# The second feed-forward of a two-layer network, computed as one quad over all 1024 tokens with a down projection of its own

## The chip, the cores and the metric

The kernel runs on one core of a Trainium2 chip. The metric is the device time of one execution in microseconds (us), the median of several runs. The profiler's trace of one execution gives the *span*, from the first to the last instruction. The engines are TensorE (PE, with its weight loads as PEld), VectorE (DVE), ScalarE (ACT), GpSimd (POOL) and SyncE (SP), which issues nearly all DMA transfers. SBUF is the on-chip memory, PSUM the accumulators that TensorE writes, DRAM the memory off the core.

## What is computed

Two layers, each with a mixing part and a gated feed-forward, and a norm at the end:

```python
    for layer in range(DEPTH):
        ...
        h = h + g1 * o_lat
        h = h + g2 * swiglu(rms_norm(h, norm_g[layer, 1]) * (1.0 + sc2) + sh2,
                            ffn_w_gate[layer], ffn_w_up[layer], ffn_w_down[layer])
        ...
    return rms_norm(h, final_g)
```

`h` is 1024 tokens by 1024 features in float32. `swiglu(x)` is `(silu(x Wg) * (x Wu)) Wd` with 2816 hidden units. Only the second layer's feed-forward, the last thing before the final norm, is changed in earnest.

## The kernel before

**Float32 by three products.** A float32 operand is *cut* into two halves: ACT casts the high half (`split` and `cut`, the cast) and DVE subtracts it to get the low half (names that end in `l`). `mm3` (lines 155 to 157) then issues three matmuls for one: high by high, high by low, low by high.

**Seven products for eight.** Gate and up projections are taken over two by two blocks by Winograd's form of Strassen's identity. A is the weight, in blocks of 128 hidden units by 512 input features (gate and up side by side); B is the normed input, in blocks of 512 features by half of the tokens. Four weight combinations S1 to S4 and four input combinations T1 to T4 are formed. One *step* takes a pair of hidden tiles (2 x 128 units; `NP` = 11 pairs), does the products A11 B11, S2 T2, A12 B21, S3 T3, S1 T1, A22 T4 and S4 B22, adds them up on DVE into the four blocks C, and `hidden` multiplies silu(gate) by up.

**Two token groups.** In the second feed-forward `FF = Quad(1, h, 256, ...)` goes over 512 tokens at a time: `X0` holds the operands of tiles 0 to 3, `X1` those of tiles 4 to 7. A token half is 256 columns, so a product is 24 matmuls of 256 columns. There are `NS` = 22 steps: the weights of all 11 pairs are loaded by SP, combined on POOL (`form`, lines 1312 to 1321, written in place over the raw blocks) and cut (`cut`, line 1327) once for each group. Six cuts of a step have their low half on DVE, that of A22 on POOL. The operands of `X1` (norm, transposes by TensorE, the T combinations and seven cuts) are made in `side1` during the steps 7 to 10 of the first group.

**The down projection inside the step.** `downs` of step s - 1 runs in the middle of step s: 4 token tiles x 2 column halves x 2 hidden tiles x 3 = 48 matmuls of 512 columns. Each pair of down weights is loaded as `wd`, multiplied by the gain `g2` on POOL (line 1302) and cut. DVE adds the PSUM tile `pd` to `h` (line 1364), which stays in SBUF.

**Before and behind.** The layer's gated mixing output (`pgl` matmuls of 512 columns, lines 2020 to 2037) comes just ahead. `ahead` starts the feed-forward's operands in its last quarter. Behind the last step `finish_row` takes the row norm and writes the output, one token tile at a time.

**Order.** Every engine works through its own instructions in order, and a wait holds up all that stand behind it. A scheduler sets this order when the program is built, by what depends on what and its own costs; SP's queue of transfers is one of those orders.

Of the kernel before, what the change touches and what calls it, by code (L numbers as in the profile page):

```python
# [11 lines left out]
F32 = mybir.dt.float32  # L12
# [8 lines left out]
P = 128  # L21
# [70 lines left out]
def build_(tc, A, out):  # L92
# [61 lines left out]
    def mm3(o, ah, al, bh, bl, first, last):  # L154
        nc.tensor.matmul(o, ah, bh, start=first, stop=False)  # L155
        nc.tensor.matmul(o, ah, bl, start=False, stop=False)  # L156
        return nc.tensor.matmul(o, al, bh, start=False, stop=last)  # L157
# [1274 lines left out]

    mix_evac(8, 0, early[0])
# [300 lines left out]
    # context: final state of both directions by pairwise combination  # L1734
# [136 lines left out]
    # within-chunk part  # L1871
# [121 lines left out]
    hp = popen("h", "right")  # L1993
    h = [hp.tile([P, D], F32, name=f"hb{i}") for i in range(8)]
    for i in range(8):
        nc.sync.dma_start(h[i], hdram[i])
    xpa = popen("ffxA", "right")
    FF = Quad(1, h, 256, xpa, popen("raw", "right"))
    X0 = ColumnOperands(FF, (0, 1, 2, 3), True)
    X1 = ColumnOperands(FF, (4, 5, 6, 7), False)  # L2000
    def ahead(i, part):
        if (i, part) == (3, 1):
            FF.load(0)
            X0.prep()
        if (i, part) == (4, 1):
            X0.column(0, gp)
            X0.column(1, gp)
            FF.form(0, "S3")
            FF.form(0, "S2")
        for k in {(5, 0): (0, 1), (5, 1): (2, 3), (6, 0): (4, 5), (6, 1): (6, 7)}.get((i, part), ()):  # L2010
            X0.turn(k)
            if k < 6:
                X0.column(k + 2, gp)
        if (i, part) == (6, 0):
            X0.cut("B11")
            X0.form("T1", nc.vector)
        if (i, part) == (7, 0):
            X0.form("T2", nc.vector)
            X0.form("T3", nc.gpsimd)
            X0.cut("B21")  # L2020
            X0.form("T4", nc.gpsimd)

    for cb in range(4):
# [18 lines left out]
        wl_ = wn  # L2042
    pclose("glu")
    pclose("ssmA")
# [1 line left out]
    FF.begin()  # L2046
    FF.g2 = FF.fq.tile([P, D], F32, name="g2r")
    nc.sync.dma_start(FF.g2, row(1, 5, 0))
# [92 lines left out]
```

## Time and profile before

| | before |
|---|---|
| time, median of 3 runs | 2802.89 us (2801.14 to 2805.78) |
| span of the profiled execution | 2800.7 us |
| busy: PE, DVE, POOL, ACT | 2551.2, 2062.8, 1256.8, 1109.9 us |
| mean granted TensorE clock | 0.962 |
| second feed-forward: last `pgl` matmul to the end | 2042.5 to 2800.7 us, 758.2 us |

The span is one execution and 2.2 us under the median of the runs. A busy time is a sum over the whole program and says nothing of one stage, so the stages are read one by one below. Granted clock 1.00 is full speed.

### The profile page before, as it was taken

What the parts mean: (1) busy time and instruction counts of PE and PEld (TensorE: products, weight loads), DVE (VectorE), ACT (ScalarE), POOL (GpSimd) and SP (SyncE); (2) the same over time, 40 slices, a digit from 0 to 9 for tenths busy, and PEclk for the clock granted to TensorE, in tenths of its full rate; (3) what the DMA queues carried; (4) which work ended last, traced back from release to release, by engine and by line L of the source; (5) the groups of instructions that cost most, each with busy time, mean ns of one, the idle gap of its engine ahead of it and who ended that gap; (6) DMA issues with size and microseconds to landing.
All of it is one profiled execution on the core that took longest, in us unless ns stands there. A gap on an engine that the chain in (4) does not pass through costs nothing.

```text
span 2800.7 us, 40131 instructions
## 1 busy us (share of the span) xinstructions
PE 2551.2 (91%) x15300; PEld 2208.7 (79%) x15300; DVE 2062.8 (74%) x3302; ACT 1109.9 (40%) x1944; POOL 1256.8 (45%) x1084
## 2 busy tenths in 40 slices
PE   7999999988998989889999976499989999889998
PEld 4788777777887879778888863398879998789997
DVE  3545786797888778797766869822298889888887
ACT  4242662363433434333323391421243345443343
POOL 1212111334665654566434567411155554665553
PEclk9999999999999999989999997799999999999999
DMA  6731345333333324433364247441032222233222
GB/s 242 196 104 45 108 138 164 98 126 137 112 107 99 120 86 167 156 100 105 98 186 149 82 161 235 156 143 61 1 98 98 99 91 91 83 121 106 91 97 70
DMA packets 262338, 330.84 MB, mean 118 GB/s; under 512 B 67713, under 2 KB 197553, under 8 KB 261761
## 3 DMA queue, kind: packets, MB, share of 16 engines
q1 hardware_dynamic: 259008, 318.51, 35.2%
q0 software_dynamic: 3136, 9.77, 1.1%
q8 instruction: 120, 1.97, 0.3%
q14 instruction: 74, 0.60, 0.1%
HBM read 285.22 MB, written 48.12 MB: 119 GB/s over the span
## 4 chain that ended last, share of the span: by engine, by line
PE 47%; DVE 33%; ACT 7%; POOL 5%; issue 5%; DMA 3%; SPq 0%; ACTq 0%; POOLq 0%; DVEq 0%
PE pd L155 5%; PE pd L156 5%; PE pd L157 5%; DVE sg L1350 5%; POOL wr L1318 3%; DVE SA L1861 3%; DVE hidl L152 2%; DVE S2l L1327 2%; PE pft L1960 2%; PE pgl L157 2%; PE pgl L156 2%; PE pgl L155 2%; PE pS L157 2%; PE pS L155 2%; DVE A12l L1327 2%
## 5 line engine op out<-in xcount | busy, mean ns | idle before, releaser
L1312 POOL TENSOR_TENSOR ws<-wr 128x1024 f32<-128x1024 f32 x42 | 108.3, 2578 | 251.2 <-DVE S1l L1327 170.0
L1318 POOL TENSOR_TENSOR wr<-wr 128x1024 f32<-128x1024 f32 x40 | 96.3, 2408 | 276.9 <-DVE A11l L1327 276.9
L1327 ACT CAST S4h<-wr 128x1024 fp32r<-128x1024 f32 x43 | 45.1, 1049 | 421.7 <-PE pd L157 421.7
L155 PE MATMUL pd<-W0h,hidh 128*128 128x512 f32 x396 | 163.3, 412 | 47.3 <-DVE c L1396 30.9
L1350 DVE TENSOR_TENSOR sg<-sg,c 128x320 f32<-128x320 f32 (+1 forms) x176 | 191.4, 1088 | 4.9 <-ACT sg L1349 4.6
L1302 POOL TENSOR_TENSOR wd<-wd,g2r 128x1024 f32<-128x1024 f32 x66 | 185.1, 2825 | 16.4 <-DMA wd<-in_ffn_w_down 16.4
L149 ACT CAST hidh<-sg 128x320 fp32r<-128x320 f32 (+1 forms) x176 | 75.9, 432 | 243.0 <-DVE sg L1350 242.9
L1321 POOL TENSOR_TENSOR wr<-wr 128x1024 f32<-128x1024 f32 x42 | 110.3, 2626 | 125.0 <-DVE A12l L1327 121.5
L156 PE MATMUL pd<-W1l,hidh 128*128 128x512 f32 x396 | 158.7, 401 | 5.2 <-DVE W1l L1327 5.2
L156 PE MATMUL pd<-W0l,hidh 128*128 128x512 f32 x396 | 158.7, 401 | 3.1 <-DVE W0l L1327 3.1
L1364 DVE TENSOR_TENSOR hb<-hb,pd 128x512 f32<-128x512 f32 x176 | 115.8, 681 | 59.2 <-PE pd L157 58.9
L155 PE MATMUL pd<-W1h,hidh 128*128 128x512 f32 x396 | 158.2, 400 | 0.1
L157 PE MATMUL pd<-W1h,hidl 128*128 128x512 f32 x396 | 158.2, 399 | 0.0
L157 PE MATMUL pd<-W0h,hidl 128*128 128x512 f32 x396 | 158.0, 399 | 0.0
L152 DVE TENSOR_TENSOR hidl<-sg,hidh 128x320 fp32r<-128x320 f32 (+1 forms) x176 | 136.4, 776 | 20.1 <-ACT hidh L149 20.0
L1327 DVE TENSOR_TENSOR S2l<-wr,S2h 128x1024 fp32r<-128x1024 f32 x42 | 85.7, 2039 | 80.9 <-ACT S2h L1327 80.9
L155 PEld LDWEIGHTS pd<-W0h,hidh 128*128 128x128 f32 x396 | 77.2, 195 | 72.3 <-DVE c L1396 36.6
L1349 ACT ACTIVATE sg<-c 128x320 f32<-128x320 f32 (+1 forms) x176 | 78.0, 444 | 119.2 <-DVE c L1392 60.5
L157 PE MATMUL pS<-xT3h,S3l 128*128 128x320 f32 (+1 forms) x352 | 108.6, 308 | 12.8 <-DVE S3l L1327 12.8
L1327 POOL TENSOR_TENSOR A22l<-wr,A22h 128x1024 fp32r<-128x1024 f32 x42 | 104.9, 2498 | 21.9 <-PE ada L227 15.3
L155 PE MATMUL pS<-xT2h,S2h 128*128 128x320 f32 (+1 forms) x352 | 108.2, 307 | 7.0 <-DVE c L1424 7.0
L155 PE MATMUL pA<-xB21h,A12h 128*128 128x320 f32 (+1 forms) x352 | 107.8, 306 | 5.2 <-DVE c L1429 5.2
(691 smaller groups left out, 9314.9 us busy)
## 6 DMA issues: line engine op xcount, KB each, us to landing
wd<-in_ffn_w_down SPq DMA_DIRECT2D x88, 512.0 KB
wr<-in_ffn_w_gate SPq DMA_DIRECT2D x86, 512.0 KB
wr<-in_ffn_w_up SPq DMA_DIRECT2D x86, 512.0 KB
mw<-in_mod_w SPq DMA_DIRECT2D x80, 512.0 KB
ftab<-tF SPq DMA_DIRECT2D x32, 256.0 KB
etab<-tpar SPq DMA_DIRECT2D x32, 256.0 KB
El<-etab SPq DMA_DIRECT2D x16, 512.0 KB
wl_s<-in_ssm_glu_w SPq DMA_DIRECT2D x32, 256.0 KB
```

Source lines behind the costliest of these rows:

```text
L152: nc.vector.tensor_sub(lo, src, hi.bitcast(F32))
L155: nc.tensor.matmul(o, ah, bh, start=first, stop=False)
L156: nc.tensor.matmul(o, ah, bl, start=False, stop=False)
L157: return nc.tensor.matmul(o, al, bh, start=False, stop=last)
L1302: nc.gpsimd.tensor_mul(t, t, self.g2)
L1312: return eng.tensor_add(b(n), *((b("A21"), b("A22")) if place else (b("S2"), b("A11"))))
L1318: return eng.tensor_sub(b(n), b("A22"), b("S3"))
L1321: return eng.tensor_sub(b(n), b("A12"), b("S2"))
L1327: r = nc.scalar.copy(hi, src), (low or nc.vector).tensor_sub(lo, src, hi.bitcast(F32))
L1350: nc.vector.tensor_mul(tmp, tmp, c[:, 1])
L1364: nc.vector.tensor_add(self.h[t][:, cs], self.h[t][:, cs], pd)
L1861: eng.tensor_add(cur, cur, tm[:, b])
```

## The change

The second feed-forward becomes a class `Feed`. The parts:

- **One quad over all 1024 tokens.** A token half is now 512 columns, a product 24 matmuls of 512 columns into a pair of PSUM banks, and there are 11 steps. Weights are loaded, formed and cut once. The low half of A22 is cut on DVE too. The first A11 and A12 products of steps 0 and 1 run ahead of step 0 (`open_step`, `close_step`), with the 32 transposes of the second token half between them; those of the first half stay in the `pgl` stage.
- **No down projection in the step.** The hidden blocks are kept as operands of seven products more: POOL makes the four combinations (last lines of `step`), SP stores all seven blocks to DRAM (`hd`). `turn_down` loads a pair of down weights (1 MB), POOL makes their four T combinations, SP stores these to DRAM (`td`). The multiplication of the weights by `g2` is gone.
- **A down phase.** `down` does the seven products one after the other over the 11 hidden pairs: 7 x 11 x 12 = 924 matmuls of 512 columns. For each two hidden pairs `next_raw` loads 1 MB (`hd` and weights or `td`; three buffers `rr`, the first two loads into the old weight buffers `wr0` and `wr1`), `next_cut` casts on ACT and subtracts on DVE. As 11 is odd, each product ends with a half-sized load.
- **h goes through DRAM.** `tile_done` stores the finished rows of `h` to `hdram` and scales them in place for the transposes (on SP the last of these stores stands ahead of the loads of step 1's weights); `hf` reloads them after the last step, together with `g2r`; `gained` multiplies by `g2`, adds to `hf`, and does the final norm by row.
- Beside these, the scratch memory of GpSimd's own DMA queue is set to 2048 bytes, and the scheduler has a few instructions of the *first* feed-forward's opening in another order on DVE and ACT.

```diff
+        def product(self, s, n, o, first, last, side={}):
+            hi, lo = (w.rearrange("p (k q) n -> p k q n", q=2) for w in self.op.pop((s, n)))
+            xh, xl = self.x[self.PAIR[n]]
+            for q in range(2):
+                for k in range(4):
+                    mm3(o[:, q], hi[:, k, q], lo[:, k, q], xh[:, k], xl[:, k], first and k == 0, last and k == 3, skip_group_check=True)
+                    if 4 * q + k in side:
+                        side[4 * q + k]()
...
+        def turn_down(self, s):
+            t = self.left.tile([P, 2, 2, 512], F32, name="wd", tag="wd", bufs=1)
+            nc.sync.dma_start(t.rearrange("p a h n -> p a (h n)"), self.Wd[:, :, s].rearrange("a p n -> p a n"))
+            e = nc.gpsimd
+            b11, b12, b21, b22 = t[:, 0, 0], t[:, 0, 1], t[:, 1, 0], t[:, 1, 1]
+            e.tensor_sub(b11, b12, b11)
+            e.tensor_sub(b12, b22, b12)
+            e.tensor_sub(b22, b22, b11)
+            e.tensor_sub(b21, b21, b22)
+            for n, v in enumerate((b11, b22, b12, b21)):
+                nc.sync.dma_start(self.td[n, s], v)
+
+        def step(self, s):
...
+            Y = self.pair("Y")
+            self.product(s, "S2", Y, True, False)
+            u = self.ctile()
+            p1 = self.c[s][0]
+            nc.vector.tensor_add(u, p1, Y)
+            if whole:
+                self.cut(s, "S3")
+                self.close_step(s, "X")
+            c11 = self.c.pop(s)[1]
+            self.cut(s, "S1")
...
+            self.product(s, "S3", Y, False, False)
+            v = self.ctile()
+            nc.vector.tensor_add(v, p1, Y)
+            self.cut(s, "A22")
...
+            e = nc.gpsimd
+            h11, h12, h21, h22 = c11[:, 1], p1[:, 1], u[:, 1], v[:, 1]
+            e.tensor_add(v[:, 0], h21, h22)
+            e.tensor_sub(c11[:, 0], v[:, 0], h11)
+            e.tensor_sub(u[:, 0], h11, h21)
+            e.tensor_sub(p1[:, 0], h12, c11[:, 0])
+            self.store(s, "S1", v)
...
+            self.turn_down(s)
+        def next_cut(self):
...
+            for a in range(2):
+                hi = wp.tile([P, 2, 512], F32R, name="dh", tag="wh", bufs=4)
+                lo = wp.tile([P, 2, 512], F32R, name="dl", tag="wl", bufs=4)
+                nc.scalar.copy(hi[:, 0:m], t[:, a, 0:m])
+                nc.vector.tensor_sub(lo[:, 0:m], t[:, a, 0:m], hi[:, 0:m].bitcast(F32))
...
+        def down(self, gained):
...
+                for k in range(0, NP, 2):
+                    self.next_raw()
+                    self.next_cut()
+                    (H, W_), m = self.cutq.pop(0)
+                    for kk in range(m):
+                        for i in range(4):
...
+                    elif n == 5:
+                        nc.vector.tensor_add(v[i], v[i], o[i])
+                        gained(4 + i, 1, v[i])
...
+    for s in range(NP):
+        FF.step(s)
+    FF.begin_down()
...
+    hf = [fin.tile([P, D], F32, name=f"hf{i}") for i in range(8)]
+    for i in range(8):
+        nc.sync.dma_start(hf[i], hdram[i])
...
+    def gained(i, q, src):
+        cs = slice(512 * q, 512 * q + 512)
+        tmp = fin.tile([P, 512], F32, name="ftmp", tag="ftmp", bufs=2)
+        nc.vector.tensor_mul(tmp, src, g2[:, cs])
+        (nc.vector if q else nc.gpsimd).tensor_add(hf[i][:, cs], hf[i][:, cs], tmp)
+        square(i, q)
+        if q:
...
+            nc.vector.scalar_tensor_tensor(o_, hf[i], rs[:, 0:1], fg, op0=ALU.mult, op1=ALU.mult)
+            nc.sync.dma_start(ov[:, i, :], o_)
+
+    FF.down(gained)
```

**POOL in the steps.** Before, one step's stretch of POOL's order holds four combinations of gate and up weights (L1312 to L1321), the low half of A22 and the two multiplications of `wd` by `g2`:

```order
L1312 TENSOR_TENSOR ws_20800<-wr 128x1024
L1315 TENSOR_TENSOR wr<-wr 128x8x128
L1327 TENSOR_TENSOR A22l<-wr,A22h 128x1024
L1318 TENSOR_TENSOR wr<-wr 128x8x128
L1302 TENSOR_TENSOR wd<-wd,g2r 128x1024 x2
L1321 TENSOR_TENSOR wr<-wr 128x8x128
```

Of the change, this is a stretch of one of the early steps, from one formation of S1 (`ws`) on. L1499 are the other formations, L1555 to L1558 the four T combinations of a down weight, L1617 to L1620 the four combinations of the hidden blocks `c`:

```order
L1495 TENSOR_TENSOR ws_19039<-wr 128x1024
L1499 TENSOR_TENSOR wr<-wr 128x8x128 x2
L1555 TENSOR_TENSOR wd<-wd 128x512
L1556 TENSOR_TENSOR wd<-wd 128x512
L1557 TENSOR_TENSOR wd<-wd 128x512
L1558 TENSOR_TENSOR wd<-wd 128x512
L1499 TENSOR_TENSOR wr<-wr 128x8x128
```

Behind these rows come another set of four on `wd`, the four on `c`, and a third set on `wd`, and then the next S1. The scheduler has moved the 11 sets of `turn_down` into the first steps: two sets stand in the stretch of step 0, three in each of the next three, and none from then on.

**SP between the two phases.** Before, nothing stands between the last loads of down weights and the stores of the output:

```order
L1292 DMA wr<-in_ffn_w_gate 128x4x256
L1292 DMA wr<-in_ffn_w_up 128x4x256
L1300 DMA wd<-in_ffn_w_down 128x1024 x4
L2067 DMA out_dram<-of 128x1024 x4
L2137 UNCONDITIONAL_BRANCH
```

Of the change, these rows stand around the last step's stores of the hidden blocks (`hd`); `rr` are the loads of the down phase, of which two pairs stand ahead of these rows:

```order
L1546 DMA hd_16876<-c 128x2x512 x2
L1548 DMA hd_16876<-c 128x512
L1546 DMA hd_16876<-c 128x2x512
L2369 DMA g2r<-mdram 128x1024
L2372 DMA hf_20857<-hdram 128x1024
...
L2372 DMA hf_20864<-hdram 128x1024
L1648 DMA rr<-hd_16876 128x2x512
L1654 DMA rr<-in_ffn_w_down 128x2x512
```

The third load of the down phase stands behind the last step's stores, behind `g2r` and behind all eight loads of `hf`.

**DVE at the last change of products in the down phase.** Before, the tail of the program on DVE adds `pd` to `h` and ends each row by one norm instruction (`of`):

```order
L1364 TENSOR_TENSOR hb_16884<-hb_16884,pd 128x512
L283 RECIPROCAL rf4rs<-rf4rs 128x1
L2066 SCALAR_TENSOR_TENSOR of<-hb_16883,rf4rs,fg 128x1024
L281 TENSOR_SCALAR rf5rs<-rf5ss 128x1
L1364 TENSOR_TENSOR hb_16885<-hb_16885,pd 128x512
```

Of the change, the end of `gained` for the tiles 4 to 7 and the next cuts (`dl`) of the last product:

```order
L2382 TENSOR_TENSOR ftmp<-dv_20885,g2r 128x512
L283 RECIPROCAL rf4rs<-rf4rs 128x1
L283 RECIPROCAL rf5rs<-rf5rs 128x1
L2383 TENSOR_TENSOR hf_20864<-hf_20864,ftmp 128x512
L2390 SCALAR_TENSOR_TENSOR of<-hf_20861,rf4rs,fg 128x1024
L2390 SCALAR_TENSOR_TENSOR of<-hf_20862,rf5rs,fg 128x1024
L2387 TENSOR_TENSOR rfss<-ssq 128x1 x2
L1666 TENSOR_TENSOR dl<-rr,dh 128x1024
```

The row work of four token tiles (adds, multiplications, two of the four norm instructions) stands ahead of the cut of the last product's second load.

## Rows read from the trace of the kernel before

**Rows 1.** The page: span, busy time of each engine (us, share).

```profile
span 2800.7 us, 40131 instructions
PE 2551.2 (91%) x15300; PEld 2208.7 (79%) x15300; DVE 2062.8 (74%) x3302; ACT 1109.9 (40%) x1944; POOL 1256.8 (45%) x1084
```

**Rows 2.** Stages of the second feed-forward: busy time by engine, clock, DMA.

```profile
core 0: us, PE busy (x) PEld busy (x) DVE busy (x) ACT busy (x) POOL busy (x), PEclk, DMA share, GB/s
2042.60:2110.50 67.90, 57.87 (x385) 53.87 (x384) 61.23 (x55) 27.96 (x37) 41.48 (x16) 0.92 0.36 117
2142.40:2296.00 153.60, 151.03 (x1035) 140.14 (x1034) 127.67 (x153) 61.49 (x95) 83.95 (x33) 1.00 0.29 97
2296.00:2489.00 193.00, 173.36 (x1145) 159.32 (x1144) 173.19 (x182) 96.54 (x157) 118.64 (x45) 0.96 0.29 93
2489.00:2750.00 261.00, 253.11 (x1745) 235.25 (x1745) 213.30 (x252) 100.63 (x147) 146.78 (x59) 1.00 0.30 99
```

**Rows 3.** PE's timeline: matmuls of 512 columns (27 steps), then of 256 (24 steps).

```profile
1919.70 0.39 PE L157 MATMUL pgl<-wl_h,yC 128*128 128x512 f32 x1
...
1925.82 0.39 PE L157 MATMUL pgl<-wl_h,yC 128*128 128x512 f32 x1
...
2110.52 0.28 PE L155 MATMUL pA<-xB11h,A11h 128*128 128x256 f32 x1
...
2113.40 0.28 PE L155 MATMUL pS<-xT2h,S2h 128*128 128x256 f32 x1
```

**Rows 4.** The chain that ended last: cuts of A11, one a step.

```profile
2104.16 1.23 DVE A11l L1327
...
2136.03 1.23 DVE A11l L1327
...
2295.56 1.24 DVE A11l L1327
...
2488.98 1.15 DVE A11l L1327
```

**Rows 5.** PE's waits from 2042 to 2111 us: in total, times, longest.

```profile
PE pS L157 <- DVE S4l L1327: 2.6, 1, 2.6
```

**Rows 6.** Groups by line, engine, operation and shape: count, busy us, mean ns.

```profile
L1327 DVE TENSOR_TENSOR A12l<-wr,A12h 128x1024 fp32r<-128x1024 f32 x6 | 7.3, 1212 | 0.0
L1327 DVE TENSOR_TENSOR S2l<-wr,S2h 128x1024 fp32r<-128x1024 f32 x6 | 14.0, 2337 | 14.8 <-ACT S2h L1327 14.8
L1327 ACT CAST A12h<-wr 128x1024 fp32r<-128x1024 f32 x6 | 6.2, 1034 | 0.0
L1370 DVE TENSOR_TENSOR hr<-hr,pd 128x1024 f32<-128x1024 f32 x55 | 66.7, 1218 | 60.4 <-PE pd L157 60.4
L1315 POOL TENSOR_TENSOR wr<-wr 128x1024 f32<-128x1024 f32 x6 | 14.4, 2398 | 0.5
L779 POOL TENSOR_TENSOR q_l<-t,t 128x512 f32<-128x512 f32 x7 | 9.1, 1301 | 78.3 <-DVE t L777 78.3
L1150 POOL TENSOR_TENSOR xB<-xB,xB 128x1024 f32<-128x1024 f32 x2 | 6.8, 3408 | 0.3 <-ACT xB L1130 0.3
```

**Rows 7.** Tiles sg and c, 2110 to 2295 us: least, median and most ns.

```profile
L1350 DVE TENSOR_TENSOR sg<-sg,c x24: 408/412/2622, 2111.3 to 2284.5; 128x256 f32<-128x256 f32 x24
L1424 DVE TENSOR_TENSOR c<-c,pA x6: 674/675/675, 2113.9 to 2273.1; 128x512 f32<-128x512 f32 x6
```

**Rows 8.** Stretches early in the program with the DMA engines full.

```profile
15.00:20.00 5.00, 5.00 (x20) 1.06 (x16) 0.28 (x1) 0.00 (x0) 0.00 (x0) 1.00 1.05 387
25.00:30.00 5.00, 2.11 (x5) 1.68 (x6) 4.13 (x8) 2.11 (x3) 2.55 (x2) 0.67 1.05 387
30.00:35.00 5.00, 5.00 (x16) 2.49 (x15) 0.44 (x1) 0.00 (x0) 0.00 (x0) 0.64 0.37 136
```

**Rows 9.** Timeline of the end: last matmul, last norm instruction.

```profile
2792.73 0.39 PE L157 MATMUL pd<-W1h,hidl 128*128 128x512 f32 x1
2795.77 1.28 DVE L2066 SCALAR_TENSOR_TENSOR of<-hb,rf7rs,fg 128x1024 f32<-128x1024 f32 x1
```

More of the change, by code (lines that the diff above doesn't have):

```diff
@@ L152, in split, with mm3 @@
         nc.vector.tensor_sub(lo, src, hi.bitcast(F32))
[L154 to L157, printed above, removed]
+    def mm3(o, ah, al, bh, bl, first, last, **kw):
+        nc.tensor.matmul(o, ah, bh, start=first, stop=False, **kw)
+        nc.tensor.matmul(o, ah, bl, start=False, stop=False, **kw)
+        return nc.tensor.matmul(o, al, bh, start=False, stop=last, **kw)
     @contextlib.contextmanager
@@ L2001, in ahead, with turn @@
+    def turn(k, half):
+        pt = bank(name="nGpt")
+        for n in range(4):
+            nc.tensor.transpose(pt[:, n * P:(n + 1) * P], h[4 * half + n][:, k * P:(k + 1) * P], ident)
+        FF.modulate(k, half, pt)
     def ahead(i, part):
+        if part == 1:
+            tile_done(i)
         if (i, part) == (3, 1):
             FF.load(0)
[L2004 to L2007, printed above, removed]
-            FF.form(0, "S3")
-            FF.form(0, "S2")
@@ L2010, in ahead @@
[L2010 to L2021, printed above, removed]
+        if i == 5 or i == 6:
+            k = 4 * (i - 5) + 2 * part
+            turn(k, 0)
+            turn(k + 1, 0)
@@ L2023, in build_ @@
+        if (i, part) == (5, 0):
+            FF.form(0, "S1")
+            FF.form(0, "S3")
+        if (i, part) == (6, 0):
+            FF.cutx("B11")
+        if (i, part) == (7, 0):
+            FF.cutx("B21")
+            FF.cut(0, "A11")
+            FF.form(0, "S2")
     for cb in range(4):
@@ L2095, in build_ @@
-    FF.cut(0, "A11")
-    FF.cut(0, "A12")
-    with after(*last):
-        t2 = X0.cut("T2")
-    with after(*t2, last[2]):
-        FF.cut(0, "S2")
-        t3 = FF.cut(0, "S3")
-        FF.form(0, "S1")
-    with after(*t3):
-        t3 = X0.cut("T3")
-    with after(*t3):
-        X0.cut("T1")
-    FF.form(0, "S4")
-    prev = None
-    for s in range(NS):
-        X = X0 if s < NP else X1
-        FF.step(s, X, prev, side1)
-        prev = X
-    FF.cut(NS - 1, "W0", nc.gpsimd)
-    FF.cut(NS - 1, "W1")
@@ L2115, in build_ @@
-    FF.downs(NS - 1, prev, lambda t: finish_row(t, finish_stats([t])[:, 0:1]))
+    FF.b["B12"], FF.b["B22"] = FF.raw("B12"), FF.raw("B22")
+    FF.load(1)
+    FF.cut(1, "A11")
+    FF.open_step(0, "X")
+    FF.cut(0, "A12")
+    FF.form(0, "S4")
+    FF.open_step(1, "Z", {n: (lambda k=n - 3: turn(k, 1)) for n in range(3, 8)})
+    FF.cut(1, "A12")
+    FF.form(1, "S1")
+    FF.form(1, "S3")
+    FF.close_step(0, "X", {n: (lambda k=n + 5: turn(k, 1)) for n in range(0, 3)})
+    FF.formx("T1")
@@ new lines, in build_ @@
+    FF.formx("T2")
+    FF.cutx("T2")
+    FF.cut(0, "S2")
+    FF.close_step(1, "Z")
+    FF.formx("T3")
+    FF.cut(0, "S3")
+    FF.cutx("T3")
+    for s in range(NP):
+        FF.step(s)
+    ov = out[0].rearrange("(c j) d -> c j d", j=8)
+    FF.begin_down()
+    fin = FF.dr_
+    fg = fin.tile([P, D], F32, name="fg")
+    nc.sync.dma_start(fg, bass.AP(tensor=A["final_g"].tensor, offset=A["final_g"].offset, ap=[[0, P], [1, D]]))
+    g2 = fin.tile([P, D], F32, name="g2r")
+    nc.sync.dma_start(g2, row(1, 5, 0))
```

276 lines of the change are left out of this document (223 added, 53 removed).

## The prediction, made before the kernel was run

> **What bounds the kernel now.** The page says that TensorE is busy for 91% of the span [rows 1], but that is an average over stages, so I read the second feed-forward by itself, in stages [rows 2]. In its steady steps (2142 to 2296 and 2489 to 2750 us) PE is busy for 97 to 98% of the time at a granted clock of 1.00. Two stages are worse: the first 67.9 us, with 57.9 us busy, and 2296 to 2489 us, with 173.4 of 193 us busy while DVE is busy for 173 us: there the second token group's operands are made. What PE pays for a matmul is its distance to the next start, not the length shown: 27 steps of 512 columns take 1925.82 - 1919.70 = 6.12 us, 0.2267 us each, and 24 of 256 columns take 2.88 us, 0.120 us each [rows 3]. So the stage's matmuls need 22 steps x 168 x 0.120 = 443.5 us for gate and up and 22 x 48 x 0.2267 = 239.4 us for down, 682.9 of 758.2 us. The other 75.3 us are stalls. The chain of waits shows where: A11 is cut every 31.87 us in the steady part (2104.16 to 2136.03), where matmuls fill 20.16 + 10.88 = 31.04 us, but the five steps from 2295.56 to 2488.98 take 193.4 us, 34 us more than five steady ones [rows 4]. In the opening two steps' products and one `downs`, 40.3 + 10.9 = 51.2 us, take 67.9 us: 16.7 us lost, with PE waiting for low halves from DVE (S4l for 2.6 us at once) [rows 2, 5]. After the last matmul 7.7 us go to the end (2792.96 to 2800.7) [rows 9].
>
> **The sum for PE.** After the change there are 11 x 7 x 24 = 1848 matmuls of 512 columns in the steps, 418.9 us (38.1 us a step), and 924 in the down phase, 209.5 us. Together 628.4 us, 54.5 us less than before: seven products for eight in the down projection save 132 matmuls, 29.9 us, and 512 columns at 0.2267 us against two of 256 at 0.240 us save the rest. The 34 us of the second group's operands go too, since that group no longer stands inside running steps; its 32 transposes cost PE some 4.1 us in the opening instead (a transpose has 128 columns, so from half of 0.120 us to the whole 0.2267 with its own weights: 2 to 7 us; I take 0.13 each). From here everything is a question of what new stalls eat of the 88 us.
>
> **Opening.** As before, PE waits for cuts. There are twice the cuts of operands (14 of 128 x 1024 instead of 7), but each product covers 5.44 us instead of 2.88, so the proportion stays. New is that A11 of step 1 waits for weights that SP may load only behind the store of tile 7, and tile 7 needs its gated product first: about 2 us of DVE and POOL work, then 2.5 MB at 387 GB/s [rows 8], 4 us of it before A11. I take 18 us, near the 16.7 of before; 10 if the wider cover helps, 28 if the 12 cuts and subtractions of the opening go at 2.34 instead of 1.21 us [rows 6].
>
> **DVE and POOL in the steps.** Low cuts cost 1.21 us, but 2.34 us beside POOL (S2l); a multiplication `sg` that reads two SBUF operands takes 0.41 us at its best and 2.62 at its worst, and an add that reads PSUM takes 0.674 to 0.675 us always [rows 6, 7]. So these two kinds of work exclude each other, and their times add. DVE has seven cuts and three multiplications of 512 (0.61, half a cut), 10.3 us a step; POOL has four formations of 2.40 and four combinations of 128 x 512 at 1.30 (L779), 14.8 us, and 5.2 us for each set of down weights. With no set that is 25 us of 38.1, with one 30, but with three sets, in three of the early steps, 40.7. The excess, 3 x 2.6 = 8 us, falls on POOL, whose S1 and S3 stand a step ahead, so I put 3 us on the path (0 to 8; the adds from PSUM, 1.22 us, are not touched). The Trainium skill's page on SBUF (SBUF — State Buffer, "Who interferes with whom") has it as a rule: a DVE instruction with two SBUF inputs and a GpSimd one that reads SBUF share a port pair, an exclusive lock for the whole instruction. By that rule the excess is these 8 us; were the ports only shared in bandwidth, DVE's 20 and POOL's 30.4 us would both fit in 38.1 and it would be nothing. The trace agrees with the lock: S2l's 2.34 us is a cut and most of another engine's instruction. Elsewhere the next step's cuts have 38 us, and PE waits 0.
>
> **Step 1.** Here A11 and A12 have run already, so only 5.44 us lie between the end of step 0 and the product S3 of step 1, which must wait until DVE has added S2 into `u`. `u` needs a free `c` buffer: all six are held until the first hidden combination of step 0 is stored. Step 0's last add, silu and multiplication end some 3.5 us after its last product. But on POOL the second set of down weights (three instructions) stands ahead; the first set ends, behind two formations (4.8 us) and weights loaded behind the cut of S4, some 4 us before the end of step 0, and its stores and the next load (1 MB, 2.7 us and its landing) take until 3 us after it. So the combination comes at 3 + 4 x 1.30 = 8 us, its store 3.65 us later (the last output store took 2800.7 - 2797.05 = 3.65) [rows 9], the add of 1.22 us at 13. PE waits 13 - 5.4 = 8 us (3 to 13).
>
> **Between the phases.** Before, the two projections alternated and nothing lay between. Now the cuts of the first two pairs are ready, 10.9 us for PE after the last step (time T). The third pair's load stands behind the last hidden stores (add 1.2, silu and multiplication 1.2, four combinations of 1.30: T + 8), behind `g2r` and `hf`. From T + 4 some 1.8 + 4.7 + 1.0 = 7.5 MB move; at 387 GB/s that is 19.4 us [rows 8]. Landing, cast 1.03 and cut 1.21 [rows 6]: T + 28 or so. PE waits 17 us, and an idle PE starts at a low clock: where it waited for full DMA engines early in the program, the granted clock was 0.67 and 0.64 for the next 10 us [rows 8]; I add 2. Forecast 19 us, 10 if `hf` overtakes less, 28 if transfers run at 300 GB/s.
>
> **Down phase.** A pair of hidden tiles is 1 MB for 5.44 us of PE, 193 GB/s. In the steady steps a DMA share of 0.30 carried 99 GB/s [rows 2], 330 at full share, so it is fed. Its cuts, 2 x 1.03 on ACT and 2 x 1.21 on DVE, fit. At a change of products the half-sized load covers only 2.7 us, against 1.03 + 2 x 1.21 = 3.5: about 1.1 us at each of six changes. Two cost more. From the fifth to the sixth DVE has four multiplications between adds and cuts (3.5 us in all). From the sixth to the seventh it has, ahead of the second load's cut, four adds (0.67), four multiplications and four adds (0.61 each, 7.6 us together), the small ones, two norm instructions (1.28) [rows 6, 7, 9]: about 14 us from the first bank's end, then two cuts, 17; PE has 2.0 + 5.4 us. 9.5 us. Sum 4 x 1.3 + 3.5 + 9.5 = 18 (10 to 24).
>
> **Tail.** Behind the last matmul DVE does for four rows add, multiplication, add, norm instruction and small ones, 0.67 + 0.61 + 0.61 + 0.5 + 1.28 = 3.7 us, 14.7 in all, of which 1 is done when PE ends; with 3.65 us for the store 17 us against 7.7 (15 to 20).
>
> **Sum** against the span: 2042.5 + 418.9 + 4.1 + 18 + 3 + 8 + 19 + 209.5 + 18 + 17 = 2758.0. The profiled execution is 2.2 us under the median, so **2760 us**, 43 us less (ratio 0.985). The reordered few instructions of the first feed-forward I put at 0 (3 either way: PE's order there is unchanged).
>
> **Rivals.**
> *The stalls are hidden.* If opening, step 1, the passage and the changes of products all come at their low ends (10, 3, 10, 10, no lock excess), the time is 2760 - 8 - 5 - 9 - 8 - 3 = 2727. For it: PE's cover per cut doubles. Against: POOL's and SP's orders, which put late work ahead.
> *The stalls at their upper ends*: 2760 + 10 + 5 + 5 + 9 + 6 + 3 = 2798, just about no change; half of it is 2780.
> *POOL becomes the bound*, the way to slower. If POOL's instructions stretch as its slowest did (3.41 for 2.40, 1.42 times [rows 6]), an early step's sum is 30.4 x 1.42 + 10.3 = 53.5 us instead of 38.1, 46 us over three steps, of which all falls on PE once S1 and S3 have lost their step of lead: 2760 + 43 = 2803. It decides from some 14 us a step in these three. Against: in the steady steps the formations took 2.40 us beside DVE's cuts, and it was DVE that was stretched.
> *The down phase is bound by DMA.* 40.4 MB in 209.5 us: only under some 160 GB/s would it cost 43 us. The rows speak of 330.
>
> **Chances.** My forecast 0.55; hidden stalls 0.15; upper ends 0.18 (of which a third within 0.2%); POOL 0.07; DMA 0.05. A measurement here can tell 0.2%, 5.6 us. Faster by more: 0.88, within: 0.05, slower: 0.07. The range runs from the hidden case to just under the upper ends: 2730 to 2790.
>
> **What would show it.** In the changed profile: up steps 38.1 us apart with PE near full; an early POOL stretch with almost no idle time, S2l or other cuts at 2.3 us; PE waiting at S3 of step 1 for a DVE add that waits for a store; a gap near T + 11 of some 17 us that ends with a DVE cut of `rr`, with DMA at its fullest; two gaps of nearly 5 us behind the sixth down product; last matmul to end 17 us. I would be wrong if steps came 42 us apart or more, if loads of `rr` landed later than PE's 5.44 us, or if `hf` did not hold up the third load.

## The result, and the profile after

The change makes the kernel slower: 2817.89 us (median of 4 runs, 2809.91 to 2824.37) against 2802.01 us (four runs; the 2802.89 us above was the median of three of them), ratio 1.0056 with a 95% interval of 1.0036 to 1.0076. The forecast was 2760 us. The page of the changed kernel, span and busy times:

```profile
span 2808.0 us, 35665 instructions
PE 2499.3 (89%) x13320; PEld 2079.7 (74%) x13320; DVE 1805.4 (64%) x2910; ACT 1027.0 (37%) x1745; POOL 1095.1 (39%) x1059
```

Every engine has less to do than in [rows 1]. So the time went into waits, and the stages say where (columns as in [rows 2]):

```profile
2041.00:2101.80 60.80, 40.89 (x153) 30.46 (x152) 48.34 (x36) 35.91 (x43) 23.87 (x8) 0.78 0.21 69
2101.80:2166.00 64.20, 52.12 (x217) 41.88 (x218) 33.02 (x26) 11.37 (x14) 36.37 (x21) 0.89 0.48 172
2166.00:2315.00 149.00, 127.97 (x530) 102.08 (x529) 66.36 (x48) 30.75 (x36) 98.67 (x57) 0.93 0.56 194
2315.00:2543.00 228.00, 228.00 (x984) 184.34 (x983) 109.39 (x98) 63.45 (x73) 84.84 (x43) 1.00 0.29 97
2543.00:2573.00 30.00, 11.78 (x50) 9.14 (x49) 4.85 (x5) 4.16 (x5) 5.06 (x4) 0.76 0.80 293
2573.00:2792.40 219.40, 204.96 (x876) 164.98 (x875) 116.69 (x130) 83.78 (x111) 14.38 (x8) 0.99 0.51 175
2792.40:2808.00 15.60, 0.22 (x1) 0.00 (x0) 11.53 (x26) 3.59 (x12) 0.00 (x0) 0.67 0.34 134
```

The rows are the opening, steps 0 and 1, steps 2 to 4 with the start of step 5, the rest of the steps, the passage, the down phase and the tail. The late steps are what was forecast: PE never idle. The third row is not, and no engine but PE is busy there for more than two thirds of the time. Set against the prediction's sum, with the distance of PE's starts as the measure, the 50 us between its span of 2758.0 us and this one of 2808.0 are found in full, term by term. This execution was the fastest of the four, 8 us under their median, and where those 8 us went is not known.

| term | forecast, us | measured, us | more |
|---|---|---|---|
| start of the stage | 2042.5 | 2041.0 | -1.5 |
| opening stalls | 18 | 29.5 | 11.5 |
| S3 of step 1 | 8 | 14.2 | 6.2 |
| stalls in steps 3 to 5 | 3 | 26.9 | 23.9 |
| matmuls of the steps, distance | 0.2267 each | 0.2315 | 8.4 |
| passage | 19 | 22.3 | 3.3 |
| changes of products | 18 | 17.5 | -0.5 |
| tail | 17 | 15.5 | -1.5 |

**Steps 3 to 5.** The waits stand behind the first product of each of these steps (the expectations below count them to the steps before, 2 to 4). POOL's timeline from the last combination of step 2's hidden blocks into step 4 (start, length, and in brackets the idle time before and what ended it):

```profile
2238.93 1.29 POOL L1620 TENSOR_TENSOR c<-c 128x512 f32<-128x512 f32 x1
2253.99 1.29 POOL L1555 TENSOR_TENSOR wd<-wd 128x512 f32<-128x512 f32 x1 [13.77 <-DMA wd<-in_ffn_w_down]
...
2259.34 2.34 POOL L1495 TENSOR_TENSOR ws<-wr 128x1024 f32<-128x1024 f32 x1
2261.64 4.66 POOL L1499 TENSOR_TENSOR wr<-wr 128x1024 f32<-128x1024 f32 x2
```

POOL stands idle for 13.8 us before the third set of down weights, whose load may only be issued when the set before has left the one buffer `wd`. Behind the set stand the formations. S2 is the first of the two instructions in the last row (it ends at 2263.98 us; the second is S3 of the next step), and these are the rows of ACT, DVE and PE that wait for it:

```profile
2264.01 1.04 ACT L1505 CAST S2h<-wr 128x1024 fp32r<-128x1024 f32 x1 [24.39 <-POOL wr L1499]
2265.09 2.28 DVE L1506 TENSOR_TENSOR S2l<-wr,S2h 128x1024 fp32r<-128x1024 f32 x1 [20.94 <-ACT S2h L1505]
2268.97 1.21 DVE L1602 TENSOR_TENSOR c<-c,pY 128x1024 f32<-128x1024 f32 x1
2270.32 0.77 PE L155 MATMUL pY<-xT2h,S2h 128*128 128x512 f32 x1 [11.31 <-DVE c L1602]
```

PE's row names the add of step 3 that frees bank Y. That add was not slow: it stands behind S2l in DVE's order, S2l behind ACT's cast, the cast behind POOL, and POOL behind a load. In the 149 us of the third row POOL waits five times for such a load, 4.5 to 13.8 us at a time and 40.0 us together. Of PE's 26.9 us, 3.6 are not waits but 18 matmuls behind them at the lower clock, 0.427 us apart. From A11 to A11 steps 3 and 4 take 48.3 and 52.9 us (42 was the sign by which I would be wrong). SP's queue at the same place:

```profile
2241.17 3.01 SPq L1560 DMA_DIRECT2D td<-wd  x4
2248.43 0.38 SPq L1552 DMA_DIRECT2D wd<-in_ffn_w_down  x1
2249.22 0.38 SPq L1486 DMA_DIRECT2D wr<-in_ffn_w_gate  x1
```

The load of `wd` goes out 7 us after the first store of the set before, POOL can start on it 5.6 us later, and the next weights (`wr`) stand behind it.

**Step 1.** DVE's add into `u`, and POOL ahead of it:

```profile
2132.19 1.26 POOL L1555 TENSOR_TENSOR wd<-wd 128x512 f32<-128x512 f32 x1 [8.99 <-DMA wd<-in_ffn_w_down]
2136.09 1.26 POOL L1617 TENSOR_TENSOR c<-c 128x512 f32<-128x512 f32 x1
2140.57 1.22 DVE L1574 TENSOR_TENSOR c<-c,pY 128x1024 f32<-128x1024 f32 x1 [8.52 <-DMA hd<-c]
```

The mechanism is the one predicted (a full set of `c` buffers, the hidden combinations behind three instructions of the second set); the second set's weights landed 8 us after the end of step 0 (2124.2 us), where I had put 3.

**Opening.** DVE and POOL, 2072 to 2092 us:

```profile
2072.63 3.44 DVE L1470 TENSOR_TENSOR rawT<-rawB,rawB 128x1024 f32<-128x1024 f32 x1
2075.99 3.43 DVE L1506 TENSOR_TENSOR S3l<-wr,S3h 128x1024 fp32r<-128x1024 f32 x1
2079.35 3.42 DVE L1470 TENSOR_TENSOR rawT<-rawB,rawB 128x1024 f32<-128x1024 f32 x1
2082.68 3.37 DVE L1478 TENSOR_TENSOR xT2l<-rawT,xT2h 128x1024 fp32r<-128x1024 f32 x1
...
2075.06 3.27 POOL L1499 TENSOR_TENSOR wr<-wr 128x1024 f32<-128x1024 f32 x1
2078.29 3.39 POOL L1470 TENSOR_TENSOR rawB<-rawB,rawT 128x1024 f32<-128x1024 f32 x1
```

Six instructions of DVE, for whose last ones PE waits, take 3.4 us each and not 1.2, in strict turns with POOL's. Another part of the 29.5 us is the clock: it was granted at 0.78 in this stretch, for 0.92 in the opening before [rows 2], and 30 matmuls stand 0.427 us apart, 6.0 us more than at 0.2267. The prediction had a term for the clock in the passage alone.

**Passage and tail.** The third load's way, PE's first matmuls behind it, and the last instruction of DVE:

```profile
2552.65 5.61 SPq L2372 DMA_DIRECT2D hf<-hdram  x8
2559.49 0.37 SPq L1648 DMA_DIRECT2D rr<-hd  x1
...
2569.90 1.04 ACT L1665 CAST dh<-rr 128x1024 fp32r<-128x1024 f32 x1 [24.75 <-DMA rr<-hd]
...
2572.36 0.79 PE L155 MATMUL pd<-dh 128*128 128x512 f32 x1 [18.22 <-ACT dh L1665]
2573.61 0.79 PE L156 MATMUL pd<-dl,dh 128*128 128x512 f32 x1 [0.47 <-DVE dl L1666]
2574.21 0.63 PE L157 MATMUL pd<-dh,dl 128*128 128x512 f32 x1
2574.63 0.63 PE L155 MATMUL pd<-dh 128*128 128x512 f32 x1
...
2803.02 1.28 DVE L2390 SCALAR_TENSOR_TENSOR of<-hf,rf3rs,fg 128x1024 f32<-128x1024 f32 x1
```

The third load stands behind eight of `hf`, with the DMA engines at 0.80. After 18 us without work PE starts at the lower clock: 11 matmuls 0.427 us apart, 2.2 us more.

**Distance of matmuls.** PE's timeline in a step without waits:

```profile
2414.98 0.40 PE L155 MATMUL pY<-xT4h,A22h 128*128 128x512 f32 x1
2420.58 0.39 PE L155 MATMUL pZ<-xB22h,S4h 128*128 128x512 f32 x1
2426.13 0.39 PE L155 MATMUL pX<-xB11h,A11h 128*128 128x512 f32 x1
```

24 matmuls of A22 take 5.60 us, 0.2333 each, and those of S4 5.55, where 0.2267 [rows 3] would give 5.44. A step takes 39.0 us, not 38.1, with nothing to wait for.

### The profile page after: what moved, and what is told of

It reads as the page before. It is cut to its first block, busy times and chain, and to the rows that moved or that the text cites. A ratio compares the mean times of both kernels' runs of the same rounds, so it can differ in the third digit from the quotient of the medians.

```text
span 2808.0 us, 35665 instructions
## 1 busy us (share of the span) xinstructions
PE 2499.3 (89%) x13320; PEld 2079.7 (74%) x13320; DVE 1805.4 (64%) x2910; ACT 1027.0 (37%) x1745; POOL 1095.1 (39%) x1059
## 4 chain that ended last, share of the span: by engine, by line
PE 48%; DVE 26%; POOL 8%; DMA 6%; issue 6%; ACT 5%; SPq 1%; POOLq 0%; DVEq 0%; ACTq 0%
PE pd L155 4%; PE pd L156 4%; PE pd L157 4%; DVE SA L2134 3%; DVE sg L1350 2%; PE pft L2233 2%; PE pgl L156 2%; PE pgl L155 2%; PE pgl L157 2%; DVE scan L2130 2%; DMA wr<-in_ffn_w_up 1%; DVE tF L607 1%; DVE tF L608 1%; PE pS L155 1%; PE ptp L877 1%
## 5 line engine op out<-in xcount | busy, mean ns | idle before, releaser
L1666 DVE TENSOR_TENSOR dl<-rr,dh 128x1024 fp32r<-128x1024 f32 (+1 forms) x84 | 96.3, 1181 | 100.4 <-ACT dh L1665 100.0
L155 PE MATMUL pd<-dh 128*128 128x512 f32 x308 | 121.8, 395 | 20.5 <-ACT dh L1665 18.2
L1665 ACT CAST dh<-rr 128x1024 fp32r<-128x1024 f32 (+1 forms) x84 | 78.5, 979 | 157.7 <-PE pd L156 113.1
L156 PE MATMUL pd<-dl,dh 128*128 128x512 f32 x308 | 122.2, 397 | 12.2 <-DVE dl L1666 12.2
L1327 ACT CAST S4h<-wr 128x1024 fp32r<-128x1024 f32 x21 | 22.1, 1051 | 275.1 <-PE pd L157 275.1
L157 PE MATMUL pd<-dh,dl 128*128 128x512 f32 x308 | 120.9, 392 | 0.0
L1318 POOL TENSOR_TENSOR wr<-wr 128x1024 f32<-128x1024 f32 x20 | 48.2, 2409 | 185.8 <-DVE A11l L1327 185.8
L1499 POOL TENSOR_TENSOR wr<-wr 128x1024 f32<-128x1024 f32 x33 | 86.7, 2637 | 62.8 <-DVE A12l L1506 39.4
L1350 DVE TENSOR_TENSOR sg<-sg,c 128x320 f32<-128x320 f32 x88 | 100.5, 1143 | 3.2 <-ACT sg L1349 3.0
L1312 POOL TENSOR_TENSOR ws<-wr 128x1024 f32<-128x1024 f32 x21 | 55.9, 2661 | 116.5 <-DVE S1l L1327 96.5
L155 PE MATMUL pgl<-wl_h,yTh 128*128 128x512 f32 x256 | 100.1, 391 | 0.0
L156 PE MATMUL pgl<-wl_l,yTh 128*128 128x512 f32 x256 | 99.6, 389 | 0.0
L2134 DVE TENSOR_TENSOR SA<-SA,scan 128x48 f32<-128x48 f32 x508 | 91.3, 238 | 0.0
```

What stands on the lines that cost most here:

```text
L155: nc.tensor.matmul(o, ah, bh, start=first, stop=False, **kw)
L156: nc.tensor.matmul(o, ah, bl, start=False, stop=False, **kw)
L157: return nc.tensor.matmul(o, al, bh, start=False, stop=last, **kw)
L1312: return eng.tensor_add(b(n), *((b("A21"), b("A22")) if place else (b("S2"), b("A11"))))
L1350: nc.vector.tensor_mul(tmp, tmp, c[:, 1])
L1499: eng.tensor_sub(b(n), b(x), b(y))
```

## The experiments

Theory A says that POOL's order and the round trips of the sets in it cost the early steps; B that it is DVE and POOL excluding each other; C that the DMA engines are full. The moment at which this stage begins differs by some us from run to run (the last `pgl` matmul began between 2038.2 and 2046.7 us), so single runs are compared by their stalls.

**One set a step.** `done` is POOL's last combination of the hidden blocks of the step.

```diff
-            self.turn_down(s)
+            self.turn_down(s, done)
...
+            with after(done):
                 e.tensor_sub(b11, b12, b11)
...
```

> The changed kernel, with one edit: the four combinations of a down weight on POOL may only stand behind the four combinations of the hidden blocks of the same step, so each step holds one set instead of three in the early ones. Theory A (POOL takes its instructions in order, and three sets a step, each a round trip of a store and a load through one buffer wd, hold up the formations of the next weights): the stalls at S2 in steps 2 to 4 (about 27 us) go, and those at S3 of step 1 (14 us) shrink to 3 to 10 us; steps 39 us apart from step 2 to the end; time 2817.9 - 27 - 4 to - 11 = 2780 to 2787 us, still faster than before by about 0.6%. Rival B (the steps are slow because DVE and POOL exclude each other, the sums of both engines' time being what counts): 11 sets cost the same 5 us each wherever they stand, but spread they fit (30 of 39 us), so the early steps gain only the forecast 3 to 8 us: 2810 to 2815. Rival C (the DMA traffic of the early steps is what is late, weights behind other transfers): the traffic is spread too, so B and C need the other two runs.

Measured: 2784.92 us, ratio to before 0.9939 (0.9926 to 0.9951). Steps 3 to 5 lose nothing beyond the distance of matmuls, S3 of step 1 loses 3.9 instead of 14.2 us, and the passage 3.9 us more, since the last set's stores now stand in it: -26.9 - 10.3 + 3.9 = -33.3 us, and the medians differ by 33.0. That these two agree so closely is in part luck: the two profiled executions differ by 22.1 us only, as this one begins the stage 5.9 us later and loses 4.9 us more in the down phase, where more of its matmuls run at the lower clock. The window of steps 2 to 5:

```profile
2162.00:2320.00 158.00, 158.00 (x682) 127.71 (x681) 77.58 (x64) 42.73 (x49) 85.42 (x49) 1.00 0.45 153
```

PE is busy throughout. The 11 sets and their bytes are the same: only their places differ.

**No sets**, and **sets without POOL's part.**

```diff
-            self.turn_down(s)
...
```

> The changed kernel without the sets: no loads, combinations and stores of the down weights' combinations at all; the down phase reads blocks of the raw down weights in their place (the same bytes), so the output is not the reference's. All theories: the early stalls go; A says about as much as with one set a step, 27 us in steps 2 to 4 and 6 to 12 in step 1, time about 2775 to 2785 us; what is left at S3 of step 1 is the wait for a free c buffer alone, 2 to 8 us.

```diff
-            e.tensor_sub(b11, b12, b11)
-            e.tensor_sub(b12, b22, b12)
-            e.tensor_sub(b22, b22, b11)
-            e.tensor_sub(b21, b21, b22)
```

> The changed kernel with the loads and stores of the sets as they are, but without POOL's four combinations: the raw blocks are stored, so the output is not the reference's. DMA traffic and its round trips stay in the early steps, POOL's share goes. Theory A: steps 2 to 4 lose at most 5 us instead of 27, since POOL no longer stands in line behind the round trips; 2783 to 2795 us. Rival C (DMA traffic): steps 2 to 4 still lose 20 us or more; 2810 or more. Rival B says like A here, but not in the run with one set a step.

Measured: 2776.58 and 2780.41 us (one run each). Step 1 loses 5.7 and 6.5 us, steps 3 to 5 nothing in both. In the second the traffic of the early steps is at its fullest, and PE does not wait; the window from the end of step 1 into step 4:

```profile
2148.00:2265.00 117.00, 117.00 (x506) 94.60 (x505) 52.73 (x49) 31.70 (x36) 45.69 (x23) 1.00 0.72 246
```

A DMA share of 0.72 against 0.56 with the stalls: C falls. B falls by the run with one set a step: there POOL does the same work without a stall, and 26.9 us came back in the early steps, where B had 3 to 8. A stands: the damage is that POOL waits in line for the sets' loads with formations behind it.

**Late reloads of h.**

```diff
-    nc.sync.dma_start(g2, row(1, 5, 0))
...
-    for i in range(8):
-        nc.sync.dma_start(hf[i], hdram[i])
+    def reload(n):
+        if n == 0:
+            nc.sync.dma_start(g2, row(1, 5, 0))
+        for i in range(8):
+            if i // 2 == n - 1:
+                nc.sync.dma_start(hf[i], hdram[i])
...
                     self.next_raw()
+                    if n == 0:
+                        reload(k // 2)
```

> The changed kernel with one edit: the reloads of h (eight of 512 kB) and of g2r are spread behind the first loads of the down phase, g2r with the first and two of h with each of the next four, instead of standing ahead of the third load. Theory (the 18.4 us between the phases are the third load waiting behind 4.7 MB): what stays is the last step's hidden combinations and stores, the load's landing, a cast and a cut: 2 to 6 us at T + 11; gain 12 to 16 us less 2 us if the spread loads delay others; time 2802 to 2806 us. Rival: the third load waits mainly for the stores of the last step's blocks (add, silu, four combinations of 1.3 us on POOL, store): then 10 us or more stay and the gain is at most 8 us.

Measured: 2806.61 us, ratio to before 1.0016 (1.0006 to 1.0025). The wait falls from 18.4 to 9.2 us, with 1.0 at the second cut as before, a result between the two expectations. The edit did not do all that it says: on SP `g2r` and one of the eight `hf` still stand ahead of the third load (`rr`):

```profile
2557.81 1.17 SPq L2378 DMA_DIRECT2D hf<-hdram  x1
2559.03 0.45 SPq L1648 DMA_DIRECT2D rr<-hd  x1
```

So half of the wait was the other seven `hf`, and most of the rest is what the rival named: POOL's four combinations end 8.4 us after the last step (8 was forecast), and ACT's cast comes 6.9 us after the load is issued.

**POOL held in the opening.**

```diff
-    FF.form(1, "S1")
-    FF.form(1, "S3")
...
+    gate = nc.gpsimd.tensor_copy(sm.tile([P, 1], F32, name="gate", tag="gate", bufs=1), FF.x["T3"][1][:, 3, 0:1].bitcast(F32))
+    with after(gate):
+        FF.formx("T4", nc.gpsimd)
+        FF.form(1, "S1")
+        FF.form(1, "S3")
```

> The changed kernel with one edit: in the opening POOL may form T4 and the S1 and S3 of step 1 only behind DVE's cut of T3 (a tiny copy on POOL that reads this cut makes it wait). In the changed kernel DVE and POOL alternate there at 3.3 us an instruction, where a cut alone takes 1.22. Theory L (the two exclude each other, so POOL's early work is paid by the chain on DVE for which PE waits): DVE's six instructions before S2 and S3 of step 0 go at 1.2 to 1.5 us instead of 3.3, S2 of step 0 loses 5 to 8 us instead of 15.2; gain 7 to 10 us in the opening, of which step 1 may take back up to 4, since the hidden combinations then stand later on POOL. Rival M (DVE's chain itself is as long as PE's wait, since its instructions wait for the transposes and ACT): S2 of step 0 still loses 12 us or more.

Measured: DVE's same instructions now, in its timeline:

```profile
2076.62 1.22 DVE L1470 TENSOR_TENSOR rawT<-rawB,rawB 128x1024 f32<-128x1024 f32 x1
2077.75 1.22 DVE L1506 TENSOR_TENSOR S3l<-wr,S3h 128x1024 fp32r<-128x1024 f32 x1
2078.89 1.22 DVE L1470 TENSOR_TENSOR rawT<-rawB,rawB 128x1024 f32<-128x1024 f32 x1
2080.02 1.22 DVE L1478 TENSOR_TENSOR xT2l<-rawT,xT2h 128x1024 fp32r<-128x1024 f32 x1
```

S2 of step 0 loses 8.4 instead of 15.2 us, near L's 5 to 8 and far from M's 12: L holds there. The waits inside S2, 4.6 and 5.4 us for the low half of T2, are gone; what PE waits now, 8.3 us, stands behind S2, for an add on DVE at 2097.49 us. This add stands behind the cuts of T1 and A22, which take 3.1 and 3.4 us now, in turns with the work that POOL was held from. The Trainium skill (SBUF — State Buffer, "Who interferes with whom") has a DVE instruction with two SBUF inputs and a GpSimd one that reads SBUF exclude each other for whole instructions; these rows agree, 1.22 us alone and 3.4 in turns. But the gain was passed on: S3 of step 0 loses 2.7 us, step 1 18.6 instead of 14.2, steps 3 to 5 32.3 instead of 26.9, which I put down to POOL's work and the sets coming later. The time is 2812.14 us (one run), although the late steps take 38.1 us here: a matmul takes 0.2267 us. I had not expected that; it is followed up below.

**The early cut.**

```diff
         if (i, part) == (6, 0):
             FF.cutx("B11")
+            FF.cut(0, "A11")
...
-            FF.cut(0, "A11")
...
-        nc.sync.dma_start(hdram[i], h[i])
+        if i < 7:
+            nc.sync.dma_start(hdram[i], h[i])
...
     FF.load(1)
+    nc.sync.dma_start(hdram[7], h7)
```

> The changed kernel with two edits in the opening: the cut of A11 of step 0 stands a quarter stage earlier (with tile 6 instead of tile 7), and the store of tile 7 of h to DRAM stands behind the loads of step 1's weights instead of ahead of them. Theory: A11 of step 0 loses under 5 us instead of 3.8 + 8.1, A11 of step 1 loses 0 to 3; but S2 of step 0 waits for DVE and POOL, whose chain starts where it did, so about half of the 8 us comes back as a longer wait at S2: net gain 3 to 8 us. If all of it comes back at S2 (15 becomes 23), the opening is bound by DVE and POOL alone and these two edits are worth nothing.

Measured: 2808.76 us (one run). A11 of step 0 loses 1.4 us ahead of it and 7.2 from its start to the next product's, A11 of step 1, instead of 3.8 + 8.1 us, S2 of step 0 the same 15.3: a gain of 3 us that does not come back. The expected size was missed because the loads were not all that A11 of step 1 waits for. Counted from the last `pgl` matmul they go out 10.3 us earlier, but ACT's cast of this A11 comes only 3.4 us earlier: in ACT's order it stands behind the norm of tile 7 and the copy of the first product. PE waits 4.4 us for the cast, and within the first product only 0.5 us for a low half.

**Single banks.**

```diff
-            return ps.tile([P, 2, 512], F32, name="p" + t, tag=t, bufs=1)
+            return [ps.tile([P, 512], F32, name=f"p{t}{q}", tag=f"{t}{q}", bufs=1) for q in range(2)]
```

> The changed kernel with one edit: the pair of PSUM banks of a product is two tiles of one bank each, and the adds, casts and activations that read the pair are split into two of 512. In the changed kernel's steps a matmul of 512 columns takes 0.2315 us to the next start, in its down phase and before in all matmuls of 512 columns 0.2267. Theory P (a PSUM tile of two banks costs it): 0.2267 in the steps, 1848 x 0.0048 = 9 us less, a little of which the split adds change. Rival Q (addresses of the operands in SBUF, or the number of other engines' accesses, set it): 0.231 as before.

Measured: 5.54 to 5.60 us a product, as in the changed kernel: theory P falls. The time is 2800.51 us (one run), because the waits of the early steps are shorter (16.9 us in steps 3 to 5, 11.0 in step 1); why was not followed up.

**Offsets.** The run with POOL held differs from the changed kernel in one more thing: its tiny tile lies ahead of the weights' tiles and shifts them by 32 bytes. In the built programs the weights begin at a multiple of 64 bytes in the changed kernel and the input operands mostly 32 bytes off; before, and with POOL held, both are 32 bytes off.

```diff
+    pad = popen("pad", "right")
+    pad.tile([P, 8], F32, name="pad")
     FF.right = popen("ffr", "right")
```

> The changed kernel with one edit: 32 bytes of padding ahead of the memory pool that holds most of the input operands (xB and xT), which shifts these tiles by 32 bytes. In the changed kernel the weights' tiles begin at multiples of 64 bytes and these operands 32 bytes off; before, and in the run with POOL held (where a small tile ahead of the weights shifted them), both were 32 bytes off, and there a matmul of 512 columns took 0.2267 us. Theory R (a matmul whose moving operand and whose weights begin at different multiples of 32 bytes within 64 costs 0.0067 us more): with both at 0 the steps take 38.1 us instead of 39.0, 0.2267 in all of them, 9 us less in all, about 2809 us. Rival S (it is the input operand's own offset of 32, or something else that the other run changed): 0.2267 too if the offset alone counts, 0.2315 if neither.

Measured, A11 to S2 in PE's timeline:

```profile
2390.89 0.39 PE L155 MATMUL pX<-xB11h,A11h 128*128 128x512 f32 x1
2396.33 0.39 PE L155 MATMUL pY<-xT2h,S2h 128*128 128x512 f32 x1
```

5.44 us, 0.2267 each, in all products; R and S both allow this, and the reversed offsets below decide between them. The one run took 2809.96 us, as long as the changed kernel's profiled execution: steps 3 to 5 lose 31.8 us and step 1 15.8, 6.5 us more than there, so faster products mostly wait longer for the same round trips. The expected 2809 us, counted from the median, is met in number only.

**Everything so far**, with single banks:

> The changed kernel with the edits of the others together: one set of down weight combinations a step, late reloads of h, POOL held in the opening, the early cut, and single banks. If the gains add: 2784.9 (one set a step) - 9 (late h) - 7 (POOL held) - 5 (early cut) - 9 (single banks) = 2755 us, range 2745 to 2768, faster than before by 1.2 to 2%. If the waits in the opening replace each other: 2765 us.

Measured: 2769.99 us, ratio to before 0.9881 (0.9864 to 0.9897), just past the range. The matmuls take 0.2267 us, but 18.9 us of waits at A11 and S2 come back in the steps 6 to 9; the last two runs follow them up.

**Offsets the other way round**, and **sets spread**, with a third load of the down phase ahead of the last step's end:

```diff
+            for n in {5: (5, 6)}.get(s, (s + (s > 5),)):
+                if n < NP:
+                    self.turn_down(n, done)
...
             self.next_raw(self.right, "wr1")
+            self.next_raw(self.left, "wd")
```

> The kernel of the next run with the padding of 32 bytes added: there the weights' tiles are 32 bytes off and the input operands at multiples of 64 bytes. Theory R (different offsets cost it): 0.2333 in the products with A11, A12 and A22, where both halves differ, and steps of 39.0 us again, 9 us more than the next run. Rival S (the input operand's own offset counts): 0.2267 and steps of 38.1 us, as in the next run.

> The changed kernel with these edits: one set of down weight combinations a step (two in one step, so that the last set is done a step early), its stores behind the loads of the next weights on SP, the third load of the down phase into the buffer wd, which is then free before the last step ends, the late reloads of h, POOL held in the opening, and the early cut. All tiles are 32 bytes off, so a matmul takes 0.2267 us. By the runs so far: 2785 (one set a step) - 9 (offsets) - 9 (POOL held, early cut) - 13 (between the phases at most 5 us left) = 2754 us, range 2745 to 2764; the waits for A11 (3 to 5 us each) that stood in the run with all edits, where the next weights' load waited behind the stores of a set, should be gone.

Measured: with the padding 5.60 us for every product but S4's 5.55, 39.1 us a step: S falls, and R holds for the products in which both halves differ. The time with the padding was missed: 2760.28 us (one run), 5.7 us under the run without it and not 9 over it, as its stage begins 7.0 us earlier and its waits in the steps 6 to 9 are 8.0 us for 14.6. R is not the whole rule: S4 takes 5.55 us in the changed kernel, where only one of its three kinds of matmul has different offsets and 5.49 would follow, and the products with T1 to T3 have one kind at equal offsets here and are slow throughout. The spread sets without padding: 2765.98 us, ratio 0.9869 (0.9851 to 0.9886), a little over the range, with 4.0 + 1.0 us left of the passage and 14.6 us of waits in the steps 6 to 9. POOL and SP there:

```profile
2371.32 5.47 SPq L1571 DMA_DIRECT2D td<-wd  x4
...
2379.64 0.50 SPq L1486 DMA_DIRECT2D wr<-in_ffn_w_up  x1
...
2389.15 2.38 POOL L1496 TENSOR_TENSOR ws<-wr 128x1024 f32<-128x1024 f32 x1 [12.71 <-DMA wr<-in_ffn_w_up]
2391.50 4.72 POOL L1500 TENSOR_TENSOR wr<-wr 128x1024 f32<-128x1024 f32 x2
```

The next step's S1 (`ws`) waits for its load, with this step's S2 behind it, and the load stands on SP behind a set's stores.

**Loads first.**

```diff
+                d = self.load(s + 1)
+                if self.turned:
+                    with after(d):
+                        self.flush()          # the stores of a set
+            if s:
+                self.turn_down(s - 1, self.done)
+            if not more:
+                self.turn_down(s, self.done)
```

> The run with the sets spread once more, with another place for the stores of a set: they stand behind all loads of the next weights that SP issues in the same step (one step later than there), and the double set stands in the last step, where POOL has no formations left. In the run with the sets spread PE still lost 14.6 us in steps 6 to 9 (A11 and S2), where POOL's next S1, ahead of the current S2 in its order, waited 12 us for weights whose loads stood behind the stores of a set on SP. Theory (this order on SP is the cause): these waits go, steps 38.1 us apart from step 2 on; 2766 - 12 to - 15 = 2751 to 2754 us if the passage between the phases stays at 4 to 5 us; up to 2758 if the double set makes the third load late. Rival (it is POOL's own work, 20 of 38 us a step, or the load's landing alone): 8 us or more of the waits stay, 2760 to 2768.

Measured: 2753.88 us, ratio to before 0.9828 (0.9805 to 0.9851), 48 us faster than before and the fastest of all. The passage keeps 4.0 + 1.0 us. From step 2 to the passage PE never waits:

```profile
2155.00:2500.00 345.00, 345.00 (x1524) 285.77 (x1523) 169.64 (x144) 95.99 (x109) 189.38 (x109) 1.00 0.47 160
```

The theory holds against its rival, though the stores and the double set moved at once and their shares are not told apart.

## Why the prediction was wrong

**Right.** The number of matmuls, and 0.2267 us for those of the down phase; the passage in path and size (22.3 for 19, within its ends, the low clock 2.2 for 2), although `hf` alone was only half of its wait; the changes of products in sum (17.5 for 18), which is partly luck: the sixth cost 6.9 and not 9.5, the second 3.0 and not 1.3, and the other plain ones 0.5 to 0.95, where the prediction's own 3.5 against 2.7 us makes 0.8 and not the 1.1 and 1.3 that it goes on with; the tail (15.5 for 17). POOL and DVE exclude each other as the rows of before had shown.

**The step that failed** is "DVE and POOL in the steps", 3 us with an upper end of 8. It added up busy time, 40.7 us a step, and let the excess fall "on POOL, whose S1 and S3 stand a step ahead". Measured are 26.9 us of stalls, while POOL is busy for only 98.7 of 149 us. Left out was that a set is a round trip: store, load, four instructions, through one buffer, and POOL stands in its order until the load has landed. I had shown this order, three sets a step, and priced the round trip in step 1 alone. The lead that should have absorbed it was none for S2: S2 stands behind the next S1 in POOL's order. The experiments show this cause: the same work one set a step costs nothing (all 26.9 us back), and the same traffic without POOL's part costs nothing there either.

**Sizes that were off.** The opening, 29.5 for 18, beyond its upper end of 28: that end took 2.34 us for a stretched cut, one POOL instruction's remainder, and six in a row took 3.4; and it had nothing for the lower clock, 6.0 us. Holding POOL gave 6.8 us of S2's wait back, of which S3 took 2.5. Step 1, 14.2 for 8, upper end 13: its mechanism was right, but the second set landed 5 us later than I had put it. The distance of matmuls, 8.4 us in the steps: taken from other tiles' rows, it did not hold for tiles at other offsets.

**The rivals.** "POOL becomes the bound" gave the time nearest to the result, 2803 us, at the right place, but not its mechanism: POOL's instructions were not stretched 1.42 times over these steps but 1.16 times (against 2.40 and 1.29 us), and they were late. A rival of three round trips a step, 4 to 14 us each time POOL waits, would have been the one on the other side; it was not in the list. The late steps gained as forecast, but for 0.9 us a step. The 2753.88 us of the last run, 6 under the forecast, do not bear the forecast out: that kernel has the gains of several more edits, which the forecast did not count.

## What to carry to other kernels

Work that an in-order engine does on data that is loaded for it is priced by its round trip, not by its busy time: look at what stands behind it in that engine's order, and on the queue that its stores share. A scheduler may move work that nobody waits for to the earliest place, where it stops what is waited for; pin it behind the urgent work. A lead of one step is only there for instructions whose place in the order is ahead of every wait.

## What was not expected of the hardware

A matmul of 128 x 512 took 0.2267 us where, in the built program, its weights and its moving operand begin at the same offset within 64 bytes (both at 0, or both at 32), and 0.2333 in products of which all three kinds of matmul have them 32 bytes apart: 5.44 against 5.60 us for 24, four placements tried. The exact rule for products with one half at each offset stays open. DVE and POOL, each with two inputs in SBUF, ran in strict turns of 3.35 us for one of each, where a cut alone takes 1.2 and a formation 2.4.
